# Two MLPs of a hybrid decoder step in seven block products instead of eight, over four chunks of 272 tokens

## The chip, the cores and the metric

The kernel runs on one core of one Trainium2 chip. The metric is device time in microseconds; the lower the better. TensorE (PE in the profile) multiplies matrices into the accumulator, VectorE (DVE), ScalarE (ACT) and GpSimd (POOL) work on elements, and the queue of SyncE (SP) issues most transfers between DRAM and the on-chip memory.

## The reference

One inference step of a two-layer decoder over 1088 tokens: 1024 of a prompt and 64 of eight samples, width 1024. Layer 0 has a state-space mixer, layer 1 attention with forget gates over shared keys and values; both attend to a memory as well. Each layer ends with an MLP of inner width 4096, which is what the change is about:

```python
def rmsnorm(x, g):
    x32 = x.astype(jnp.float32)
    y = x32 * lax.rsqrt(jnp.mean(x32 * x32, axis=-1, keepdims=True) + RMS_EPS)
    return (y * g.astype(jnp.float32)).astype(x.dtype)

def sqrelu_mlp(x, w_up, w_down):
    h = jax.nn.relu(x @ w_up)
    return (h * h) @ w_down
...
        h = h + jnp.concatenate([y_main, y_mem], axis=-1) @ p["w_out"][i]
        h = h + sqrelu_mlp(rmsnorm(h, p["norm_mlp"][i]), p["w_up"][i], p["w_down"][i])
    y = rmsnorm(h, p["norm_final"])
```

Everything is 32-bit floating point.

## The kernel before

Activations lie with the channel on the partitions and the tokens along the row: `[128, 8, w]` for 1024 channels and a chunk of w tokens. There are three chunks (`CH`, line 19): 384, 384 and 320 tokens.

A product keeps 32-bit accuracy by parts. `split` (line 186) writes the operand rounded for the tensor engine, H, with ACT (line 191), and the rest, L, with DVE (line 192, POOL in some places). `mm3` (line 181) then does three matmuls, H·H, H·L and L·H, into one bank of the accumulator; all matmuls go through `mm` at line 179. `Weights` loads a block of 1024 words a partition into one of four raw places `wf` and splits it into a pair of the eight places `wr`; `wall` goes round all four.

`dense` (line 210) takes up to four output tiles of 128 channels: it loads and splits their weights, then goes chunk by chunk, tile by tile, 8 k-tiles by 3 matmuls each, and hands the bank to `evict`. Banks 0 and 1 take turns. `tick` after each tile runs work that `defer` has put off, so that a norm falls behind matmuls that are already in PE's queue.

`mlp` (line 307) runs over 8 groups of 512 hidden channels. Up: four tiles by `dense`; `ev_up` takes the relu (ACT, line 314), squares (POOL, line 315) and splits the tile into `hids`, which stay on the chip. Down: four blocks of weights, and for each chunk 8 output tiles of 4 k-tiles by 3 matmuls, added by DVE (line 329) to the residual stream `hs[c]`. In the last group the squares for the next norm are summed as the tiles come (`add_square`, line 1011), and `done` norms a finished chunk.

Before it, `out_proj` (line 299) makes the 8 tiles of the output projection in two `dense` calls; at the end of the second each chunk is normed by `norm_later` (line 260): sums of squares at once, and `rest` two tiles later, with the gains applied on DVE (line 255) and a split. After the first MLP `xn` is normed with the gains of layer 1's mixer, and `xk_later` (line 1056) norms the same chunks once more with the gains of the shared keys and values.

The order of instructions on each engine's queue comes from a scheduler that simulates the program; engines then work their queues in order. Storage is laid out by hand: `setA` holds the residual stream, `setB` and `setC` the two parts of normed activations, and `phase` gives a stage its own area, which is where `hids` lie.

Of the kernel before, what the change touches and what calls it, by code (L numbers as in the profile page):

```python
# [18 lines left out]
CH = ((0, 384), (384, 384), (768, 320))  # L19
# [25 lines left out]
def yoco_step(ctx: ExitStack, tc: tile.TileContext, I, O, upto=99, dbg=None):  # L45
# [17 lines left out]

    class Place:
        """words from lo to hi of a tile"""

        def __init__(self, tile_, lo, hi):
            self.t, self.o, self.hi = tile_, lo, hi
# [10 lines left out]
        def at(self, shape, dt=F32):  # L79
            n = math.prod(shape[1:])  # L80
            assert self.o + n <= self.hi, (shape, self.o, self.hi)
            return shaped(self.t[0:shape[0], self.o:self.o + n], shape, dt)
# [7 lines left out]
    class Ring:  # L90
        """places used in turn"""
# [8 lines left out]
    class Banks:  # L100
        """banks of the accumulator, used in turn"""
# [9 lines left out]
    F_WORDS = 720 + SET + 4 * WT + 3 * 768 + 3 * 384 + 4 * 432  # L111
    R_WORDS = 2 * SET + 8 * WT
    P_WORDS = SB_WORDS - F_WORDS - R_WORDS
    top = Place(sb.tile([128, F_WORDS], F32, name="plain", tag="plain"), 0, F_WORDS)
    rnd = Place(sb.tile([128, R_WORDS], F32R, name="rounded", tag="rounded"), 0, R_WORDS)
    phases = ExitStack()
    ctx.enter_context(phases)

    def phase(name, plain, rounded=0):
        """storage of a phase, which takes the place of the one before"""  # L120
        phases.close()
        pool = phases.enter_context(tc.tile_pool(name=name, bufs=1, reuse_waits="tile"))
        assert plain + rounded <= P_WORDS, (plain + rounded, P_WORDS)
        r = []
        for n, d in ((plain, F32), (rounded, F32R)):
            r.append(Place(pool.tile([128, n], d, name=f"{name}_{d.name}", tag=d.name), 0, n) if n else None)
        return r
# [15 lines left out]
    sq0 = top.words(3 * 768)  # L143
    sq = Ring([sq0.sub(768 * i, 768) for i in range(3)])
    rs0 = top.words(3 * 384)
    rsr = Ring([rs0.sub(384 * i, 384) for i in range(3)])
    nt0 = top.words(4 * 432)
# [11 lines left out]
    class Weights:  # L159
        """raw weights and their two parts, by turns"""  # L160
# [4 lines left out]
        def __call__(self, src, shape, e=V):  # L165
# [3 lines left out]
            SY.dma_start(out=raw, in_=src)  # L169
            split(H, L, raw, e)  # L170
# [6 lines left out]
    # ------------------------------------------------------------ helpers  # L177
# [32 lines left out]
    def dense(srcs, xs, evict, load=wall, nk=8, done=None, each=tick):  # L210
        """weights stationary, activations moving; groups of tiles run chunk by chunk"""
# [48 lines left out]
    def norm_later(h, c, gi, out, keep=None, lag=2):  # L260
        """statistics now, the rest when a few more tiles have been handed to the tensor engine"""
        w = CH[c][1]
        s1 = rms_sums(h, w)

        def rest():
            rs = rms_scale(s1, w)
            if keep is not None:
                keep[c] = rs
            out[c] = rms_apply(h, rs, gi, c)
        defer(lag, rest)  # L270

# [27 lines left out]
    def out_proj(ys, w, hs, done):  # L299
        for g in range(2):  # L300
            def ev(i, c, ps, w_, g=g):
                r = hs[c][:, 4 * g + i, :]
                V.tensor_tensor(r, ps, r, op=ALU.add)
# [3 lines left out]
    def mlp(l, hs, xs, done, each=None):  # L307
        _, ph = phase(f"mlp{l}", 0, 8 * T)
        hids = {(i, c): ph([128, 2, w], F32R) for c, (_, w) in enumerate(CH) for i in range(4)}
        ebank = Banks([2, 3, 4, 5, 6])  # L310
        for g in range(8):
            def ev_up(i, c, ps, w):
                r = nt([128, w])
                S.activation(r, ps, AF.Relu)  # L314
                G.tensor_tensor(r, r, r, op=ALU.mult)  # L315
                split(hids[i, c][:, 0, :], hids[i, c][:, 1, :], r)

            dense([I["w_up"][l, 4 * g + i] for i in range(4)], xs, ev_up)
            W = [wall(I["w_down"][l, g, i], [128, 4, 256]) for i in range(4)]
            for c, (t0, w) in enumerate(CH):  # L320
                for m in range(8):
                    H, L = W[m // 2]
                    ms = slice(128 * (m % 2), 128 * (m % 2) + 128)
                    ps = ebank([128, 512])
                    for k in range(4):
                        x = hids[k, c]
                        mm3(ps[:, :w], H[:, k, ms], L[:, k, ms], x[:, 0, :], x[:, 1, :], k == 0, k == 3)
                    r = hs[c][:, m, :]
                    V.tensor_tensor(r, ps[:, :w], r, op=ALU.add)  # L329
                    if g == 7 and each:  # L330
                        each(r, c, m)
                    tick()
                if g == 7:
                    done(hs[c], c)
# [1122 lines left out]
    for c in range(3):  # L1457
        load_ym(1, c)
# [145 lines left out]
```

## Time and profile before

| | |
|---|---|
| median of three runs | 2814.22 us (2812.74, 2817.23, 2814.22) |
| span of the profiled execution | 2812.6 us |
| PE busy | 2690.6 us (96%), 17669 matmuls |
| DVE, ACT, POOL busy | 1345.2, 944.0, 681.5 us |
| moved by DMA | 307.06 MB, mean 109 GB/s |
| first MLP, second MLP | about 440 to 1220 us, about 1970 to 2795 us of the span |

The profiled execution's own time is its span, 1.6 us under the median of the runs, so the two can be compared directly. The page gives busy time, share and number of instructions of each engine, 40 slices of the span, and the chain of work that ended last. A group's line reads: line of the kernel, engine, operation, output<-inputs, shape, count | busy time, mean duration of one in ns | idle time of that engine before them and what ended it. Matmuls overlap in the pipeline, so the price of one in a row is busy time over count, not the mean duration. In the table of stretches a column is busy time and, in brackets, the number of instructions.

### The profile page before, as it was taken

Reading aid. Unit: us, or ns where it says so; the run is one execution under the profiler, and the core shown is the slowest. Engines: PE = TensorE matmul, PEld = TensorE weight load, DVE = VectorE, ACT = ScalarE, POOL = GpSimd, SP = SyncE. Lnnn points to the kernel's source line nnn. Section 1 sums busy time; section 2 is a strip of 40 time slices with the busy share of each in tenths; the row PEclk is TensorE's granted clock in tenths of the full one; section 3 lists DMA queues with packets and bytes.
Section 4 is the critical chain, followed back from the end, with each engine's and each line's share of the span. In section 5 each row is a group of like instructions: output and inputs, shape, how many; then the busy total and the mean of one; then the engine's idle time right before and its main releaser. Section 6 shows DMA issues by size and latency. Waiting matters only on the chain.

```text
span 2812.6 us, 45335 instructions
## 1 busy us (share of the span) xinstructions
PE 2690.6 (96%) x17669; PEld 2526.0 (90%) x17669; DVE 1345.2 (48%) x2597; ACT 944.0 (34%) x1947; POOL 681.5 (24%) x776
## 2 busy tenths in 40 slices
PE   7787999999999999999999989999999999999997
PEld 6776889999999999998889766777999999999997
DVE  8899646432323232283523477785553232233225
ACT  6332533221122122244422466773232122211224
POOL 6487211110111011121101455540011011101113
PEclk9899999999999999999999999999999999999999
DMA  6435332010101111132586898885211111111101
GB/s 205 111 105 171 99 108 77 31 61 31 61 31 53 38 52 39 46 131 83 182 266 211 269 293 299 277 292 179 77 31 53 38 51 40 45 45 39 52 31 64
DMA packets 175293, 307.06 MB, mean 109 GB/s; under 512 B 42661, under 2 KB 103398, under 8 KB 173542
## 3 DMA queue, kind: packets, MB, share of 16 engines
q1 hardware_dynamic: 152486, 294.46, 32.3%
q10 hardware_dynamic: 22080, 8.92, 1.2%
q8 instruction: 139, 2.28, 0.3%
q0 software_dynamic: 512, 0.79, 0.1%
q14 instruction: 76, 0.62, 0.1%
HBM read 259.18 MB, written 44.93 MB: 108 GB/s over the span
## 4 chain that ended last, share of the span: by engine, by line
PE 81%; DVE 9%; DMA 3%; POOL 2%; ACT 2%; issue 2%; SPq 0%; POOLq 0%; ACTq 0%; DVEq 0%
PE banks L179 79%; DVE rounded L192 2%; PE banks L1327 1%; DVE plain L255 1%; ACT rounded L191 1%; DMA layer_float<-in_cache_v 1%; POOL logf_float L989 1%; DVE plain L862 1%; ACT plain L1313 1%; DMA plain<-qtscr 0%; DVE plain L870 0%; POOL rounded L192 0%; PE banks L469 0%; DVE plain L1019 0%; POOL plain L864 0%
## 5 line engine op out<-in xcount | busy, mean ns | idle before, releaser
L179 PE MATMUL banks<-rounded 128*128 128x384 f32 (+4 forms) x8918 | 1548.3, 331 | 64.8 <-ACT rounded L191 16.7
L179 PEld LDWEIGHTS banks<-rounded 128*128 128x128 f32 x8918 | 1460.2, 191 | 111.9 <-issue 22.1
L179 PE MATMUL banks<-mlp_float32r,rounded 128*128 128x384 f32 (+1 forms) x4608 | 769.7, 328 | 0.0
L179 PEld LDWEIGHTS banks<-mlp_float32r,rounded 128*128 128x128 f32 x4608 | 763.1, 188 | 1.1
L191 ACT ACTIVATE rounded<-plain 128x1024 fp32r<-128x1024 f32 (+6 forms) x379 | 306.6, 821 | 784.8 <-PE banks L179 675.7
L315 POOL TENSOR_TENSOR plain<-plain 128x384 f32<-128x384 f32 (+1 forms) x192 | 202.6, 1055 | 1390.6 <-ACT plain L314 1276.8
L329 DVE TENSOR_TENSOR plain<-banks,plain 128x384 f32<-128x384 f32 (+1 forms) x384 | 204.6, 533 | 382.1 <-PE banks L179 382.1
L192 DVE TENSOR_TENSOR rounded<-plain,rounded 128x1024 fp32r<-128x1024 f32 (+4 forms) x252 | 293.8, 1172 | 152.1 <-ACT rounded L191 149.7
L192 DVE TENSOR_TENSOR mlp_float32r<-plain,mlp_float32r 128x384 fp32r<-128x384 f32 (+1 forms) x192 | 102.8, 535 | 485.0 <-ACT mlp_float32r L191 485.0
L314 ACT ACTIVATE plain<-banks 128x384 f32<-128x384 f32 (+1 forms) x192 | 89.7, 467 | 289.5 <-PE banks L179 286.0
L192 POOL TENSOR_TENSOR rounded<-plain,rounded 64x512 fp32r<-64x512 f32 (+5 forms) x127 | 144.7, 1148 | 163.0 <-ACT rounded L191 160.2
L191 ACT ACTIVATE mlp_float32r<-plain 128x384 fp32r<-128x384 f32 (+1 forms) x192 | 97.4, 507 | 211.6 <-POOL plain L315 211.6
L179 PE MATMUL banks<-layer_float 128*32 128x256 f32 (+2 forms) x1104 | 98.2, 370 | 11.2 <-ACT layer_float L1149 4.3
L192 DVE TENSOR_TENSOR rounded<-banks,rounded 128x512 fp32r<-128x512 f32 (+2 forms) x136 | 85.9, 636 | 25.3 <-ACT rounded L191 23.6
L191 ACT ACTIVATE rounded<-banks 128x512 fp32r<-128x512 f32 (+2 forms) x136 | 74.8, 559 | 57.9 <-PE banks L1327 32.9
L1317 POOL TENSOR_SCALAR plain<-plain 128x640 f32<-128x640 f32 (+6 forms) x96 | 71.4, 747 | 77.9 <-DVE plain L1316 39.1
L179 PE MATMUL banks<-rounded,layer_float32r 128*128 128x256 f32 x480 | 87.6, 299 | 2.5 <-ACT rounded L191 1.4
L1313 ACT ACTIVATE plain<-banks,plain 128x512 f32<-128x512 f32 (+2 forms) x144 | 82.3, 576 | 17.8 <-DVE plain L1310 9.5
L179 PEld LDWEIGHTS banks<-rounded,layer_float32r 128*128 128x128 f32 x480 | 68.9, 190 | 15.5 <-ACT rounded L191 4.1
L179 PEld LDWEIGHTS banks<-layer_float 128*32 128x32 f32 (+1 forms) x1104 | 39.6, 113 | 45.6 <-issue 8.9
L1307 DVE TENSOR_REDUCE plain<-banks 128x1 f32<-128x384 f32 (+3 forms) x144 | 76.6, 550 | 6.3 <-PE banks L179 5.0
L255 DVE SCALAR_TENSOR_TENSOR plain<-plain 128x384 f32<-128x384 f32 (+1 forms) x120 | 74.9, 674 | 7.2 <-DMA ymscr<-plain 5.7
(318 smaller groups left out, 1784.8 us busy)
## 6 DMA issues: line engine op xcount, KB each, us to landing
plain<-in_cache_kT SPq DMA_DIRECT2D x128, 384.0 KB
layer_float<-in_cache_v SPq DMA_DIRECT2D x128, 384.0 KB
plain<-in_w_up SPq DMA_DIRECT2D x64, 512.0 KB
plain<-in_w_down SPq DMA_DIRECT2D x64, 512.0 KB
plain<-in_w_in SPq DMA_DIRECT2D x16, 512.0 KB
plain<-in_w_out SPq DMA_DIRECT2D x16, 512.0 KB
plain<-in_xT SPq DMA_DIRECT2D x4, 1536.0 KB
plain<-fpast SPq DMA_DIRECT2D x8, 768.0 KB
```

Of the source, the lines that this page charges most:

```text
L179: PE.matmul(out, a, b, start=first, stop=last)
L191: S.activation(H, src, AF.Copy)
L192: e.tensor_tensor(L, src, H.bitcast(F32), op=ALU.subtract)
L255: V.scalar_tensor_tensor(t[:, j, :], h[:, k, :], gains[:, gi, k:k + 1], rs, op0=ALU.mult, op1=ALU.mult)
L314: S.activation(r, ps, AF.Relu)
L315: G.tensor_tensor(r, r, r, op=ALU.mult)
L329: V.tensor_tensor(r, ps[:, :w], r, op=ALU.add)
L862: V.tensor_tensor_scan(X[:, r, a], m8, X[:, r, a], 0.0, op0=ALU.mult, op1=ALU.add)
L989: G.indirect_dma_start(out=fp[i // 8][:, 128 * (i % 8):128 * (i % 8) + 128], out_offset=None, in_=I["logf_rows"], in_offset=bass.IndirectO ...
L1307: V.tensor_reduce(st[:, i:i + 1], ps[:, :n], axis=AX.X, op=ALU.max, negate=True)
L1313: S.activation(pf[:, k0:k0 + n], ps[:, :n], AF.Exp, bias=st[:, 0:1], accum_out=st[:, 2 + i:3 + i])
L1317: G.tensor_scalar(pf[:, 0:L], pf[:, 0:L], st[:, 4:5], 0.0, op0=ALU.mult, op1=ALU.add)
```

## The change

A product of two matrices cut into 2 x 2 blocks takes eight block products; Strassen's scheme takes seven, between sums and differences of blocks. The change does this for both products of the MLP, with the hidden channels or output channels, the inner dimension and the tokens each cut in two.

- There are four chunks of 272 tokens in the whole kernel; an operand holds two of them (`g`).
- `mlp_norm` replaces `norm_later`: it stores the residual chunk to DRAM (`hmid`), norms in place, and makes from two pairs of chunks the seven moving operands, already split, which stay on the chip for all of the up stage.
- Up: 16 rounds of 256 hidden channels. `weight_ops` loads 1 MB of weights, forms four sums on POOL and splits seven operands. `seven` runs the products in turn over three pairs of banks. `to_hidden` forms the seven operands of the down stage from the four result blocks and stores them to DRAM (`hops`) through three places; the last two rounds are stored as they are (`hcnv`).
- Down: 7 blocks of 512 hidden channels by 4 sweeps of 7 products, operands read back from DRAM into eleven places; results are gathered in `H5`, on DVE and POOL. The residual comes back with POOL in blocks 1 to 4. The eighth block is done in the old way with `hcnv`, and feeds `each` and `done`.
- The gains of layer 1's mixer and of the shared keys and values are multiplied into the raw weights on POOL (`Weights`, `gain`), so there is one norm after the first MLP and `xk_later` is gone.
- The sums over the past's log-forget values run between the two halves of the output projection (`past_sums`), not after it.

The core of the diff:

```diff
-CH = ((0, 384), (384, 384), (768, 320))
+CH = ((0, 272), (272, 272), (544, 272), (816, 272))
...
             SY.dma_start(out=raw, in_=src)
+            if gain is not None:
+                G.tensor_tensor(raw, raw, gain[:, :, None].broadcast_to(shape), op=ALU.mult)
             split(H, L, raw, e)
...
+    def operands(b11, b12, b21, b22, extra, put, which=(0, 1, 2)):
+        if 0 in which:
+            put(0, b11)
+        if 2 in which:
+            put(2, b21)
+        if 1 in which:
+            V.tensor_tensor(b11, b12, b11, op=ALU.subtract)
+            V.tensor_tensor(extra, b22, b11, op=ALU.subtract)
+            put(1, extra)
+            put(3, b11)
+            V.tensor_tensor(b12, b22, b12, op=ALU.subtract)
+            put(4, b12)
+            put(5, b22)
+            V.tensor_tensor(b21, b21, extra, op=ALU.subtract)
+            put(6, b21)
...
+    def weight_ops(src, cells, sh):
+        n = turn["w"]
+        turn["w"] += 1
+        raw = raws2[n % 2]
+        raw = raw.at([128, *src[1]])
+        SY.dma_start(out=raw, in_=src[0])
+        a11, a12, a21, a22 = cells(raw)
+        at = ((0, 7, 1)[n % 3], 2, 3, 4, 5, 6, (1, 0, 7)[n % 3])
+        r = [wr[j].at([128, 2, *sh], F32R) for j in at]
+
+        def put(i, x):
+            split(r[i][:, 0], r[i][:, 1], x)
+
+        put(0, a11)
+        put(6, a22)
+        G.tensor_tensor(a22, a21, a22, op=ALU.add)
+        G.tensor_tensor(a21, a11, a21, op=ALU.subtract)
+        G.tensor_tensor(a11, a22, a11, op=ALU.subtract)
+        put(1, a11)
+        put(2, a12)
+        put(3, a22)
+        G.tensor_tensor(a12, a12, a11, op=ALU.subtract)
+        put(4, a21)
+        put(5, a12)
+        return r
+
+    def seven(lhs, rhs, nk, gs, tmp, out):
+        s1, u2, u4 = (t[:, gs] for t in tmp)
+
+        def product(i):
+            n = turn["bank"] = (turn["bank"] + 1) % 3
+            v = shaped(banks[:, 1024 * n:1024 * n + 1024], [128, 2, 512], F32)[:, :, 0:CN]
+            for g in range(gs.start, gs.stop):
+                for k in range(nk):
+                    mm3(v[:, g], *lhs(i, k), *rhs(i, g, k), k == 0, k == nk - 1)
+            return v[:, gs]
+
+        S.activation(s1, product(0), AF.Copy)
+        V.tensor_tensor(u2, product(1), s1, op=ALU.add)
+        out(0, 0, product(2), s1)
+        V.tensor_tensor(u4, product(3), u2, op=ALU.add)
+        p = product(4)
+        out(1, 1, p, u4)
+        V.tensor_tensor(u2, p, u2, op=ALU.add)
+        out(0, 1, product(5), u4)
+        out(1, 0, product(6), u2)
...
+    def mlp_norm(h, c, gi):
+        w = CH[c][1]
+        s1 = rms_sums(h, w)
+        SY.dma_start(out=hmid[c], in_=h)
...
+        def rest():
+            rs = rms_scale(s1, w)
+            for k in range(8):
+                V.scalar_tensor_tensor(x[:, k, :], h[:, k, :], gains[:, gi, k:k + 1], rs,
+                                       op0=ALU.mult, op1=ALU.mult)
...
+            operands(x0[:, 0:4], x[:, 0:4], x0[:, 4:8], x[:, 4:8], extra, put, (1,) if c % 2 else (0, 2))
+        defer(2, rest)
...
+        hl = Ring([setA[i].sub(1088 * j, 1088) for i, j in ((2, 1), (0, 0), (0, 1))])
+        def to_hidden(j, q, extra):
+            b, kp = j // 2, j % 2
+            def put(i, x):
+                t = hl([128, 2, 2, CN], F32R)
+                split(t[:, 0], t[:, 1], x)
+                SY.dma_start(out=hops[i][b][:, kp], in_=t.rearrange("p h g n -> p h (g n)").bitcast(F32))
...
+        W = up_weights(0)
+        for j in range(16):
...
+            for gs in (slice(0, 1), slice(1, 2)) if j == 0 else (slice(0, 2),):
+                def out(m, n, ps, u):
+                    x = q[m][n][:, gs]
+                    V.tensor_tensor(x, ps, u, op=ALU.add)
+                    S.activation(x, x, AF.Relu)
+                    S.activation(x, x, AF.Square)
+                seven(..., 4, gs, tmp, out)
...
+            if j < 15:
+                W = up_weights(j + 1)
+            to_hidden(j, q, tmps(sh))
...
+        for b in range(7):
+            ops = hidden(b)
+            for d in range(2):
+                W = down_weights(b, d)
+                if d == 0 and 0 < b < 5:
+                    hr = residual.at([128, 8, CN])
+                    SY.dma_start(out=hr, in_=hmid[b - 1])
+                for e in range(2):
+                    m0 = 4 * d + 2 * e
+                    def out(m, n, ps, u):
+                        h = H5[:, :, n, m0 + m, :]
+                        if b == 0:
+                            V.tensor_tensor(h, ps, u, op=ALU.add)
+                            return
+                        V.tensor_tensor(h, ps, h, op=ALU.add)
+                        G.tensor_tensor(h, h, u, op=ALU.add)
+                    seven(..., 2, slice(0, 2), [tmps(sh) for _ in range(3)], out)
+                    if 0 < b < 5:
+                        for m in range(m0, m0 + 2):
+                            hc = hs[b - 1][:, m, :]
+                            G.tensor_tensor(hc, hc, hr[:, m, :], op=ALU.add)
...
-    xk = [None] * 3
-
-    def xk_later(c):
-        xk[c] = rms_apply(hs[c], rs[c], 4, c)
```

More of the change, by code (lines that the diff above doesn't have):

```diff
@@ L258, in rms_apply @@
         return H, L
[L260 to L270, printed above, removed]
     def expacc(out, x, t, ni):
@@ L297, in dump_c, with out_proj @@
             SY.dma_start(out=dbg[name][:, :, CH[c][0]:CH[c][0] + CH[c][1]], in_=ap)
-    def out_proj(ys, w, hs, done):
+    def out_proj(ys, w, hs, done, between=None):
         for g in range(2):
+            if g and between:
+                between()
             def ev(i, c, ps, w_, g=g):
@@ L305, in out_proj @@
             dense([w[4 * g + i] for i in range(4)], ys, ev, done=(lambda c: done(hs[c], c)) if g else None)
[L307 to L334, printed above, removed]
@@ new lines, in yoco_step @@
+    hops = [dt_(f"hops{i}", [7, 128, 2, 2, 2 * CN]) for i in range(7)]
+    hcnv = dt_("hcnv", [4, 128, 2, T])
+    hmid = [dt_(f"hmid{c}", [128, 8, w]) for c, (_, w) in enumerate(CH)]
+    raws2 = [joined(wf[2 * i:2 * i + 2]) for i in range(2)]
+    turn = {"w": 0, "bank": 0}
+    xplace, Pq = [None, None], []
+    def operands(b11, b12, b21, b22, extra, put, which=(0, 1, 2)):
[13 more added lines that the diff above has]
+            put(6, b21)
@@ L599, in yoco_step @@
     mem_values_of(1, kvr, wv1)
-    norm0(1)
-    norm0(2)
+    for c in range(1, NC):
+        norm0(c)
     def tiny(dt=F32):
@@ L969, in yoco_step @@
             next(mem, None)
[L970 removed]
+        n = 34 if c < NC - 1 else 26
         for m in range(6):
@@ L1004, in yoco_step @@
         return
-    xn, rs = [None] * 3, [None] * 3
-    sums = [sq.p[2].sub(384 * (c % 2), 384) for c in range(3)]
+    xl = [joined(x).at([128, 8, T], F32R) for x in (setB, setC)]
+    xn = [[x[:, :, t0:t0 + w] for x in xl] for t0, w in CH]
+    sums = [sq.p[2].sub(384 * (c % 2), 384) for c in range(NC)]
     two = Ring(sq.p[0:2])
@@ L1050, in ev_q1, with gained @@
         SY.dma_start(out=qtscr[i0 + i][:, CH[c][0]:CH[c][0] + n], in_=t[:, 0:n])
-        if c == 2:
-            SY.dma_start(out=qsscr[i0 + i], in_=t[:, 256:320])
-    xk = [None] * 3
-    def xk_later(c):
-        xk[c] = rms_apply(hs[c], rs[c], 4, c)
-    dense([I["w_in1"][6], I["w_in1"][7]], xn, ev_qm)
+        if c == NC - 1:
+            SY.dma_start(out=qsscr[i0 + i], in_=t[:, SAM])
+    def gained(gi):
+        return lambda src, shape: wall(src, shape, gain=gains[:, gi, :])
+    dense([I["w_in1"][6], I["w_in1"][7]], xn, ev_qm, gained(1))
     fa, fr = phase("layer1", P_WORDS - 3072, 3072)
@@ L1068, in yoco_step @@
     i0 = 0
-    dense([I["w_in1"][i] for i in range(4)], xn, ev_q1, each=mem_tick)
+    dense([I["w_in1"][i] for i in range(4)], xn, ev_q1, gained(1), each=mem_tick)
     i0 = 4
-    dense([I["w_in1"][i] for i in (4, 5)], xn, ev_q1, done=xk_later, each=mem_tick)
+    dense([I["w_in1"][i] for i in (4, 5)], xn, ev_q1, gained(1), each=mem_tick)
     for _ in mem:
@@ L1179, in yoco_step @@
     for j in range(3):
-        W = [wall(I["w_vf"][j, kh], [128, 4, 260]) for kh in range(2)]
+        W = [wall(I["w_vf"][j, kh], [128, 4, 260], gain=gains[:, 4, 4 * kh:4 * kh + 4]) for kh in range(2)]
         for b in range(9):
             t0 = 128 * b if b < 8 else 960
-            c = min(t0 // 384, 2)
-            ls_ = slice(t0 - CH[c][0], t0 - CH[c][0] + 128)
+            ls_ = slice(t0, t0 + 128)
             ps = dbank([128, 512])
@@ L1256, in yoco_step @@
     for i in range(6):
-        dense([I["w_k"][i]], xk, lambda _, c, ps, w, i=i: ev_k(i, c, ps, w), each=lambda: step(RATE[1]))
-    hlr = [Ring([x[c].sub(6 * CH[c][1], 512) for c in range(3)]) for x in (setB, setC)]
+        dense([I["w_k"][i]], xn, lambda _, c, ps, w, i=i: ev_k(i, c, ps, w), gained(4), each=lambda: step(RATE[1]))
+    hlr = [Ring([x[c].sub(6 * CH[c][1], 512) for c in range(NC)]) for x in (setB, setC)]
     wfl = joined(wf[2:4])
```

248 lines of the change are left out of this document (174 added, 74 removed).

## The prediction

> **What bounds the kernel now.** I read the page first (busy shares, slices, chain), then the table of stretches, then the groups of instructions of each engine.
>
> ```profile
> span 2812.6 us, 45335 instructions
> PE 2690.6 (96%) x17669; PEld 2526.0 (90%) x17669; DVE 1345.2 (48%) x2597; ACT 944.0 (34%) x1947; POOL 681.5 (24%) x776
> ...
> GB/s 205 111 105 171 99 108 77 31 61 31 61 31 53 38 52 39 46 131 83 182 266 211 269 293 299 277 292 179 77 31 53 38 51 40 45 45 39 52 31 64
> ...
> PE 81%; DVE 9%; DMA 3%; POOL 2%; ACT 2%; issue 2%; SPq 0%; POOLq 0%; ACTq 0%; DVEq 0%
> ```
>
> PE is busy 96% of the span and 81% of the chain that ended last, so what counts is which stage gives PE less to do and whether something else then ends its waits. The two MLPs are the calm slices of the GB/s row, 7 to 17 and 29 to 40; the table of stretches shows them in microseconds:
>
> ```profile
> core 0: us, PE busy (x) PEld busy (x) DVE busy (x) ACT busy (x) POOL busy (x), PEclk, DMA share, GB/s
> ...
> 460.00:1200.00 740.00, 740.00 (x4479) 739.58 (x4478) 254.78 (x387) 174.09 (x278) 100.99 (x96) 1.00 0.14 46
> ...
> 1990.00:2760.00 770.00, 770.00 (x4648) 769.31 (x4647) 265.13 (x407) 180.48 (x287) 101.63 (x96) 1.00 0.13 42
> ```
>
> PE never stops there at full clock; DVE stands at 34%, POOL at 14%, the DMA at 46 GB/s. Only fewer or shorter matmuls shorten this, and there is room beside them. How long one matmul takes, from the groups with shapes kept apart and one row of the timeline:
>
> ```profile
> L179 PE MATMUL banks<-rounded 128*128 128x384 f32 x5184 | 960.5, 343 | 34.1 <-ACT plain L820 11.3 <-DVE rounded L192 10.3 <-ACT rounded L191 3.5
> L179 PE MATMUL banks<-mlp_float32r,rounded 128*128 128x384 f32 x3072 | 544.8, 338 | 0.0
> ...
> L179 PE MATMUL banks<-mlp_float32r,rounded 128*128 128x320 f32 x1536 | 227.5, 308 | 0.0
> ...
> 1460.63 6.04 PE L179 MATMUL banks<-rounded 128*128 128x260 f32 x48
> ```
>
> They are pipelined, so the price is busy time over count, in the MLP rows: 177.3 ns for 384 columns, 148.1 for 320, hence 0.456 ns a column, and 126.2 ns for 272. The last row gives at most 126 ns for 260 columns: short matmuls with a new stationary tile each pay no visible floor there.
>
> The Trainium skill (TensorE: Matmul & The Clock Gate, "Back-to-back issue gap") gives N / 2.4 GHz + 2.5 ns, 115.8 ns here as an estimate; its 162.5 for 384 columns is 15 ns under the trace, so the sum stays with the rows. By the page it would come out 113 us lower (10,848 matmuls by 10.4 ns).
>
> **The matmuls.** Before, each layer has 32 x 8 x 3 x 3 = 2304 up and as many down; the rows above are the down half of both layers, 772.3 us, so one layer's MLP costs 772.3. After: up 16 rounds x 7 products x 2 halves x 4 k x 3 parts = 2688, down 28 sweeps x 7 x 2 x 2 x 3 = 2352, and the eighth hidden block in the old way, 4 x 8 x 4 x 3 = 384. 5424 x 126.2 ns = 684.5: 87.8 us less a layer, if PE stays the bound. A round is 21.2 us of PE, a sweep 10.6.
>
> **What is laid on the other engines.** The rows for it:
>
> ```profile
> L192 DVE TENSOR_TENSOR rounded<-plain,rounded 128x1024 fp32r<-128x1024 f32 x172 | 214.2, 1245 | 129.4 <-ACT rounded L191 127.3 <-DMA out_v<-plain 1.1 <-PE banks L179 0.9
> L329 DVE TENSOR_TENSOR plain<-banks,plain 128x384 f32<-128x384 f32 x256 | 142.3, 556 | 307.9 <-PE banks L179 307.9
> L192 DVE TENSOR_TENSOR rounded<-banks,rounded 128x512 fp32r<-128x512 f32 x120 | 81.7, 684 | 19.6 <-ACT rounded L191 18.2
> L192 DVE TENSOR_TENSOR mlp_float32r<-plain,mlp_float32r 128x384 fp32r<-128x384 f32 x128 | 71.3, 557 | 421.0 <-ACT mlp_float32r L191 421.0
> L329 DVE TENSOR_TENSOR plain<-banks,plain 128x320 f32<-128x320 f32 x128 | 62.4, 487 | 74.1 <-PE banks L179 74.1
> ```
>
> About 1.05 ns an element and 150 ns: 272 is 0.44 us, 512 0.69, 544 0.72, 1088 1.29, from PSUM or SBUF alike. An up round on DVE: 7 products evicted (544) 5.0, 7 halves of weights split (512) 4.8, 4 subtractions and 7 splits of hidden operands (544) 7.9; 17.8 us beside 21.2 of PE. ACT:
>
> ```profile
> L191 ACT ACTIVATE rounded<-banks 128x512 fp32r<-128x512 f32 x120 | 70.7, 596 | 38.5 <-PE banks L1327 32.9 <-DVE plain L1307 2.6 <-DVE rounded L192 0.9
> ```
>
> 23 operations of 512 or 544 at 0.60 to 0.63, 14 us: covered. POOL:
>
> ```profile
> L192 POOL TENSOR_TENSOR rounded<-plain,rounded 64x512 fp32r<-64x512 f32 x48 | 61.0, 1277 | 51.8 <-ACT rounded L191 50.3 <-PE banks L179 0.5 <-DVE plain L1316 0.3
> L192 POOL TENSOR_TENSOR rounded<-plain,rounded 64x256 fp32r<-64x256 f32 x36 | 26.2, 728 | 38.5 <-ACT rounded L191 37.6
> ```
>
> Elements per partition count: 1.28 us for 512, 0.76 for 272, 1.34 for 544. A round's four weight sums are 5.1 us. A down sweep in blocks 1 to 4 has four adds into h (5.4), half of four weight sums (2.6), two residual adds (1.5): 9.5 us beside 10.6 of PE; blocks 5 and 6 have 8.0, block 0 2.6. DVE there has 7 x 0.72 + 3.5 x 0.69 = 7.4.
>
> DVE and POOL disturb each other. The timeline of the last norm:
>
> ```profile
> 2773.57 0.55 DVE L1019 TENSOR_TENSOR plain<-plain 128x384 f32<-128x384 f32 x1
> ...
> 2774.67 8.84 POOL L1483 TENSOR_TENSOR plain<-plain 128x384 f32<-128x384 f32 x8 [22.97 <-DVE plain L245]
> ...
> 2778.19 1.15 DVE L1019 TENSOR_TENSOR plain<-plain 128x384 f32<-128x384 f32 x1 [0.65 <-ACT plain L1018]
> ...
> 2779.27 0.55 DVE L329 TENSOR_TENSOR plain<-banks,plain 128x384 f32<-128x384 f32 x1
> ```
>
> The same SBUF operation takes 0.55 us alone and 1.15 beside POOL; the one that reads PSUM stays at 0.55. Lower bound for a round: no disturbance, PE's 21.2. Upper: whatever reads SBUF twice on DVE excludes POOL, 12.7 + 5.1 + 5.0 = 22.8. I take the middle, 22.0: DVE at half speed during 60% of POOL's 5.1 us plus its own stretch is 19.8, under PE, but an in-order queue at 93% will hold an eviction back at times (three pairs of banks give it two products, 6 us). A sweep of blocks 1 to 4: 10.6, or with exclusion 9.5 + 2.4 = 11.9; middle 11.2. The others 10.6, covered. Up 16 x 22.0 = 352; down 12 x 10.6 + 16 x 11.2 = 306; the last block 48.5.
>
> **Moved and added DMAs.** A round stores 7 tiles of 557 KB and loads 1 MB, 4.9 MB in 22 us = 225 GB/s; a block of down reads 7 x 1.11 + 2 + 1.1 MB in 44 us = 250. The page's slices reach 299, so bandwidth covers it. Eleven places for seven operands let four come a block early; the other three have the last sweep. The sync queue takes 8 issues a round: seven stores that wait for DVE's splits and, among them, the load of the next weights, which is late if a store ahead of it waits; it has a round and a half of lead (two raw places). If the cover of the stores fails, DVE's queue stops at a split, and behind that stand the evictions that free PE's banks: third rival.
>
> **Start of each MLP.** Before, a chunk's norm hides behind the next chunk's 16.8 us of matmuls. Now the chunk also becomes operands. The norm's pieces:
>
> ```profile
> 459.02 0.56 DVE L243 SCALAR_TENSOR_TENSOR plain<-banks,plain 128x384 f32<-128x384 f32 x1
> ...
> 460.60 3.27 DVE L255 SCALAR_TENSOR_TENSOR plain<-plain 128x384 f32<-128x384 f32 x6
> ```
>
> At 272: evictions 1.7, sums 2.6, finish 1.6, gain 8 x 0.43 = 3.5, then two splits of 1088 for an even chunk (12.0 in all), four subtractions and five splits for an odd one (21.1). 66 us of DVE against 48.4 of PE in the second half of the output projection, of which the first chunk's 12.1 brings no norm work, and the first weights' 4.8 and 3.0 of evictions come in. DVE ends near 86 us, while PE wants the last operand at 48.4 + 10.6 + 9 = 68: 18 us of stall a layer. Bounds: 3, if DVE's queue is so ordered that only the last chunk's first subtractions show; 25, if the new store of the residual (1.1 MB a chunk, which the norm must wait for because it overwrites h) is not covered by the 12 us between chunks. **Up to down**: 3 us (0 to 8), since h lies where the last stored tiles were.
>
> A layer: 18 + 352 + 306 + 3 + 48.5 = 727.5 against 772.3, 44.8 saved, 89.6 in two.
>
> **The rest.** The other dense products, 5184 - 3072 = 2112 matmuls of 384 and half as many of 320, become 4224 of 272: 533.1 - 530.8 = +2.3. Folding gains into the weights adds 20 POOL operations of about 2.3 us on the engine that the page shows least busy, and drops one norm on DVE; neither ended PE's waits: 0 (-5 to +5). Before the first MLP every chunk-wise instruction comes four times instead of three: some 20 DVE operations of the first norm at 0.15 us of fixed price more, and stores of 136 bytes a row instead of 192: +3 (-3 to +10). The running sums of the past (two scans, a copy, two subtractions on DVE, two stores on the sync queue) move between the halves of the output projection; their wait for the gathers is already in DVE's queue:
>
> ```profile
> 437.12 2.35 DVE L994 TENSOR_TENSOR_SCAN logf_float<-plain,logf_float 96x1024 f32<-96x1024 f32 x1 [5.99 <-DMA logf_float<-in_logf_rows,plain]
> ```
>
> Earlier in the queue it may hold evictions back for these 6 us once more; the gathers end when they did, so between 0 and 6 I take 0. The tail after the last matmul, 11 us long, handles 272 columns instead of 320: -2.
>
> ```profile
> 2800.56 0.82 PE L179 MATMUL banks<-plain 128*128 128x320 f32 x2 [3.38 <-DVE plain L1019]
> ```
>
> Sum: 2812.6 - 89.6 + 2.3 + 3 - 2 = 2726.3. The median of the runs is 1.6 above this execution's span: **2728 us**.
>
> **Rivals.**
> *PE keeps the bound and nothing stalls.* For: everything is under PE on paper. Against: DVE's 18 us start. Only 3 us a layer lost: 2814.2 - 2 x 84.8 + 3 = **2648**.
>
> *DVE and POOL shut each other out* (the 0.55 to 1.15 row). Rounds 22.8, sweeps 11.9: 18 + 365 + 318 + 3 + 48.5 = 752.5; 2814.2 - 39.6 + 3 = **2778**. The Trainium skill (GPSIMD Engine Reference, "Specifications") names this as one SBUF interface shared with VectorE, in contention when VectorE has two SBUF inputs; the row agrees, as PSUM operations keep their time.
>
> *The stores hold DVE: slower.* The hidden operands go through three places, and a split waits for the store three before. The nearest transfer, 512 KB:
>
> ```profile
> 1690.77 4.47 DMA plain<-qtscr
> ...
> 1745.99 5.48 DMA plain<-qtscr
> ```
>
> 5.5 plus ACT and DVE 1.35 is 6.9 us a turn, 2.3 a tile, where DVE has 1.1 us of work: 1.2 us of waiting on four to seven tiles, 4.7 to 8.2 a round, on a queue with 1.4 to spare. Rounds of 24.5 to 28; at 26 the layer costs 791.5, the kernel **2856**. It decides from a round of 24.7 us: (772.3 - 375.5 - 1.6) / 16. Against it: those waits can be filled with weight splits and evictions.
>
> **How the numbers follow.** Forecast (2690 to 2765) 0.48, no stall 0.14, exclusion 0.15, stores 0.20, others 0.03. 0.2% is 5.6 us, the spread of the runs shown (2812.74 to 2817.23). Faster 0.48 + 0.14 + 0.14, slower 0.19 + 0.02, same 0.03. 2650 to 2850 leaves out the tip of the first rival and half of the last.
>
> **What would show it.** Matmuls of 272 at 126 ns; 18 us of holes at the start of each MLP, ended by DVE; rounds of 22 us with DVE above 85%; POOL above 85% in sweeps of 11 us. Wrong, if a round is over 24.7 with DVE waiting for ACT and ACT for stores, or if matmuls of 272 cost over 135 ns.

## The result and the profile after

| | before | after | ratio |
| --- | --- | --- | --- |
| median of the runs, us | 2815.72 (2812.74 to 2817.4) | 2762.1 (2759.31 to 2765.74) | 0.9818, 95% interval 0.9801 to 0.9835 |
| span of the profiled execution, us | 2812.6 | 2759.2 | |

1.8% faster: 54 us by the medians, 53 by the spans, where 86 were forecast. The same program run once more against the kernel before gave 0.9805 (0.9789 to 0.9822), with a span of 2751.1. The page of the kernel after; the chain's shares are those of the chain that ended last:

```profile
span 2759.2 us, 54020 instructions
PE 2575.1 (93%) x20345; PEld 2404.4 (87%) x20345; DVE 2023.4 (73%) x3421; ACT 1239.9 (45%) x2544; POOL 1249.9 (45%) x1142
...
GB/s 200 109 110 165 105 122 83 82 248 229 234 241 314 208 258 266 198 157 108 147 261 218 265 303 312 305 296 159 96 88 249 230 236 238 306 238 242 280 170 65
...
PE 56%; DVE 18%; POOL 9%; DMA 8%; issue 4%; ACT 4%; another core or an unknown queue 1%; SPq 0%; POOLq 0%; ACTq 0%; DVEq 0%
```

PE lost 116 us of busy time, the span only 53, and PE fell from 81% of the chain to 56%. The calm slices of 31 to 64 GB/s are now at 208 to 314 for the most part. Where the MLP is bound, by the table of stretches of the kernel after (the start, a steady stretch of up, the middle of the passage to down, a steady stretch of down):

```profile
core 0: us, PE busy (x) PEld busy (x) DVE busy (x) ACT busy (x) POOL busy (x), PEclk, DMA share, GB/s
...
480.00:500.00 20.00, 16.12 (x121) 15.41 (x120) 20.00 (x25) 10.74 (x16) 12.53 (x4) 0.96 0.14 57
500.00:540.00 40.00, 29.79 (x155) 27.52 (x153) 39.12 (x59) 17.40 (x27) 7.32 (x4) 0.76 0.15 55
540.00:700.00 160.00, 160.00 (x1271) 159.88 (x1271) 147.60 (x196) 102.57 (x179) 49.09 (x30) 1.00 0.62 238
...
860.00:870.00 10.00, 4.35 (x23) 3.98 (x23) 1.97 (x4) 1.89 (x4) 0.00 (x0) 0.69 1.01 420
870.00:880.00 10.00, 6.96 (x34) 6.35 (x33) 1.45 (x2) 0.66 (x1) 0.00 (x0) 0.67 1.03 416
...
930.00:1060.00 130.00, 127.03 (x998) 125.00 (x997) 102.53 (x125) 32.65 (x54) 127.18 (x94) 1.00 0.64 249
```

Four regimes. At the start of the MLP (480 to 540) DVE is busy for 59.1 of 60 us and PE stands at times; in up's rounds PE never stops, and 160.00 / 1271 is 125.9 ns a matmul, with DVE at 92%; between up and down only the DMA is full; in down POOL is at 98% and PE still at 98%.

Read by sections, for the second half of the output projection and the MLP behind it. Their ends are marked in the timelines by evictions and by first copies, ACT's copies of the first product of a round or sweep:

| section, us | forecast | layer 0 | layer 1 |
| --- | --- | --- | --- |
| second half of the projection, rounds 0 and 1 (the start) | 110.4 | 119.6 | 118.9 |
| 13 rounds of up | 286.0 | 278.7 | 276.6 |
| first copy of the last round to that of the third sweep (the passage) | 44.6 | 58.7 | 57.3 |
| 26 sweeps of down | 285.2 | 281.2 | 282.2 |
| the eighth hidden block | 47.0 | 52.2 | 46.8 |
| together | 773.2 | 790.4 | 781.8 |
| before | 816.3 by rows | 809.1 | 810.2 |

The forecasts are the prediction's terms cut at these marks: 45.4 of projection, 18 of stall, two rounds of 22.0 and a product of 3; 13 x 22.0; 6/7 of a round, 3, two sweeps of 10.6 and 1.5; 10 x 10.6 + 16 x 11.2; 48.5 less the first group. In the kernel before the sections run from 439.4 to 1248.5 and from 1988.0 to 2798.2 us of its span, which the table of the time before gives only roughly. Both layers together are 26 us over the forecasts and were 13 cheaper before than the rows said; everything outside them is 6 us shorter instead of some 0.5 longer. That is the 33 us between the forecast's span, 2726.3, and 2759.2.

The passage is the term that failed. It holds 324 matmuls, 324 x 125.9 ns = 40.8 us; 17 us a layer are lost there, where the prediction had 3. Waits of PE in that place, then one of ACT, timelines of the kernel after:

```profile
862.38 1.89 PE L208 MATMUL banks<-rounded 128*128 128x272 f32 x12 [2.27 <-DMA rounded<-hops]
867.65 3.06 PE L208 MATMUL banks<-rounded 128*128 128x272 f32 x12 [3.38 <-DMA rounded<-hops]
872.93 2.16 PE L208 MATMUL banks<-rounded 128*128 128x272 f32 x12 [2.22 <-DMA rounded<-hops]
...
873.61 0.66 ACT L220 ACTIVATE plain<-plain 128x544 fp32r<-128x544 f32 x1 [11.60 <-DMA hcnv<-plain]
```

In the first layer PE waits 7.9 us for loads of operands and 5.6 for DVE and ACT, and ACT waits 11.6 for a store of the eighth hidden block. That names the transfers, not the cause: it may be their order, the amount, or what they wait for.

### The profile page after: what moved, and what is told of

It reads as the page before. It is cut to its first block, busy times and chain, and to the rows that moved or that the text cites. A ratio compares the mean times of both kernels' runs of the same rounds, so it can differ in the third digit from the quotient of the medians.

```text
span 2759.2 us, 54020 instructions
## 1 busy us (share of the span) xinstructions
PE 2575.1 (93%) x20345; PEld 2404.4 (87%) x20345; DVE 2023.4 (73%) x3421; ACT 1239.9 (45%) x2544; POOL 1249.9 (45%) x1142
## 4 chain that ended last, share of the span: by engine, by line
PE 56%; DVE 18%; POOL 9%; DMA 8%; issue 4%; ACT 4%; another core or an unknown queue 1%; SPq 0%; POOLq 0%; ACTq 0%; DVEq 0%
PE banks L208 54%; DVE rounded L221 5%; POOL plain L539 4%; DMA hops<-plain 2%; DVE plain L221 2%; DMA rounded<-hops 2%; PE banks L1558 1%; POOL plain L547 1%; ACT rounded L220 1%; POOL plain L381 1%; POOL plain L379 1%; POOL plain L380 1%; ACT plain L220 1%; POOL plain L385 1%
## 5 line engine op out<-in xcount | busy, mean ns | idle before, releaser
L208 PE MATMUL banks<-rounded 128*128 128x272 f32 (+4 forms) x11552 | 1626.2, 296 | 97.6 <-ACT rounded L220 27.7
L220 ACT ACTIVATE rounded<-plain 128x512 fp32r<-128x512 f32 (+5 forms) x575 | 384.3, 679 | 641.5 <-PE banks L208 473.2
L221 DVE TENSOR_TENSOR rounded<-plain,rounded 128x512 fp32r<-128x512 f32 (+4 forms) x520 | 490.8, 954 | 107.4 <-ACT rounded L220 103.3
L208 PE MATMUL banks<-mlp,rounded 128*128 128x272 f32 x3840 | 526.2, 292 | 18.0 <-DVE plain L536 5.4
L208 PEld LDWEIGHTS banks<-mlp,rounded 128*128 128x128 f32 x3840 | 502.1, 191 | 24.2 <-DVE rounded L221 8.0
L379 POOL TENSOR_TENSOR plain<-plain 128x512 f32<-128x512 f32 x60 | 98.5, 1642 | 709.2 <-DVE rounded L221 709.2
L539 POOL TENSOR_TENSOR plain<-plain,flex 128x544 f32<-128x544 f32 x192 | 292.0, 1531 | 42.0 <-DVE plain L538 39.3
L221 DVE TENSOR_TENSOR plain<-plain 128x544 fp32r<-128x544 f32 x212 | 209.8, 1006 | 28.0 <-ACT plain L220 21.9
L220 ACT ACTIVATE plain<-plain 128x544 fp32r<-128x544 f32 x212 | 136.6, 653 | 187.9 <-DMA hops<-plain 103.6
L538 DVE TENSOR_TENSOR plain<-banks,plain 128x544 f32<-128x544 f32 x192 | 137.7, 718 | 57.7 <-PE banks L208 54.9
L385 POOL TENSOR_TENSOR plain<-plain 128x512 f32<-128x512 f32 x60 | 101.1, 1685 | 65.6 <-DVE rounded L221 65.0
L221 POOL TENSOR_TENSOR rounded<-plain,rounded 64x512 fp32r<-64x512 f32 (+2 forms) x55 | 77.4, 1414 | 67.4 <-ACT rounded L220 61.9
L381 POOL TENSOR_TENSOR plain<-plain 128x512 f32<-128x512 f32 x60 | 101.1, 1685 | 3.0
L221 DVE TENSOR_TENSOR rounded<-banks,rounded 128x512 fp32r<-128x512 f32 (+2 forms) x136 | 86.0, 637 | 15.1 <-ACT rounded L220 13.2
L380 POOL TENSOR_TENSOR plain<-plain 128x512 f32<-128x512 f32 x60 | 93.2, 1553 | 4.7
```

Of the source, the lines that this page charges most:

```text
L208: PE.matmul(out, a, b, start=first, stop=last)
L220: S.activation(H, src, AF.Copy)
L221: e.tensor_tensor(L, src, H.bitcast(F32), op=ALU.subtract)
L379: G.tensor_tensor(a22, a21, a22, op=ALU.add)
L380: G.tensor_tensor(a21, a11, a21, op=ALU.subtract)
L381: G.tensor_tensor(a11, a22, a11, op=ALU.subtract)
```

## The experiments

Ratios are to the kernel before on the same chip in the same minutes; "passage" is the section of the table, layer 0 / layer 1.

| kernel | median, us | ratio (95%) | passage | start |
| --- | --- | --- | --- | --- |
| after, again | 2758.2 | 0.9805 (0.9789 to 0.9822) | 57.0 / 59.4 | 119.2 / 118.9 |
| loads in order | 2755.6 | 0.9802 (0.9781 to 0.9823) | 58.9 / 59.0 | 119.5 / 118.9 |
| wide rows | 2761.3 | 0.9815 (0.9794 to 0.9837) | 63.2 / 62.0 | 119.1 / 119.4 |
| plain MLP | 2820.6 | 1.0038 (1.0026 to 1.0050) | | |
| two places | 2770.6 | 0.9851 (0.9830 to 0.9871) | 61.9 / 62.7 | 118.3 / 118.4 |
| free place | 2764.2 | 0.9820 (0.9804 to 0.9836) | 59.3 / 62.4 | 119.1 / 119.0 |
| stores first | 2735.4 | 0.9721 (0.9705 to 0.9737) | 46.9 / 47.4 | 119.4 / 118.8 |
| splits on POOL | 2768.3 | 0.9835 (0.9818 to 0.9851) | 58.1 / 59.8 | 122.9 / 122.9 |
| stores first, sums on DVE | 2730.0 | 0.9717 (0.9699 to 0.9734) | 47.9 / 46.8 | 114.9 / 114.8 |
| stores first, fourth place | 2765.4 | 0.9841 (0.9823 to 0.9858) | 60.9 / 61.8 | 119.2 / 118.9 |
| both | 2756.9 | 0.9813 (0.9794 to 0.9831) | 61.8 / 61.2 | 114.9 / 115.4 |
| all, stores in order | 2732.9 | 0.9723 (0.9704 to 0.9741) | 47.7 / 45.5 | 114.9 / 115.6 |

**Is the gain the algorithm's?** The eight block products put back, all else as changed (the `mlp` of the kernel before, with its `rms_apply` norm, over four chunks).

> The four chunks of 272 tokens, the gains in the weights and everything else of the change stay, but both MLPs go by the eight block products of the kernel before, so this run is the change without Strassen's algorithm. By the prediction's terms the MLPs then cost 2 x 3.1 us more than before (3072 x 126.2 ns = 387.7 a half against 386.15), the other dense products 2.3, the front 3, the tail -2: 2816 + 9.5 = 2825 us, and Strassen's algorithm itself is worth 2825 - 2762 = 63. By the traces' milestones (front +4.9, mixer of the second layer -10.7, tail -0.9) it is 2815, and the algorithm is worth 53. Rival (the gain is not the algorithm's but that of the smaller chunks and the folded gains): 2790 or below.

1.0038: 10.7 us slower than the kernel before, by the prediction's terms 9.5. So the four chunks, the folded gains and the rest cost in sum what they were said to cost; their terms one by one were not measured. The seven products alone are worth 62 to 66 us (1.0038 less 0.9818 or 0.9805) of the 89.6 forecast, and what is missing is missing inside the MLPs.

**The order of the loads.** `after(x)` makes the scheduler issue an instruction behind x; the rest of the edit only declares `last`.

```diff
-                SY.dma_start(out=t.bitcast(F32), in_=hops[i][b])
+                with after(last[0] if b < 2 else None):
+                    last[0] = SY.dma_start(out=t.bitcast(F32), in_=hops[i][b])
```

> Undoes nothing; the seven operand loads of down's first block, and those of the second behind them, are only put into the sync queue in the order in which the sweep uses them. Theory (order): the stall between up and down comes from operands 5 and 6 and two of the next block being loaded ahead of 2, 3 and 4. The first two sweep intervals (24.9 + 18.6 us in the first layer, 23.1 + 17.8 in the second) fall to about 13 + 12, some 17 us a layer: 2762 - 34 = 2728 us. Rival (bandwidth): 7.8 MB at the 407 GB/s seen there take 19 us in whatever order; the two intervals keep a sum of 38 or more and the time stays above 2752.

The first sweep did shrink, from 24.9 to 7.6 us; the second grew to 32.1, and the passage stayed at 59. My theory fell. Timelines of this kernel, sync queue, DVE and PE:

```profile
846.76 4.88 SPq L515 DMA_DIRECT2D mlp<-hops  x4
...
860.81 15.85 SPq L477 DMA_DIRECT2D hcnv<-plain  x6
...
879.93 1.36 DVE L537 TENSOR_TENSOR plain<-banks,flex 128x544 f32<-128x544 f32 x2 [10.99 <-DMA hcnv<-plain]
...
880.71 3.09 PE L208 MATMUL banks<-mlp,rounded 128*128 128x272 f32 x12 [14.00 <-DVE plain L537]
```

Now one row says what the order hid. PE waits 14.0 us for DVE, and DVE 11.0 us for a store of the eighth hidden block: its sums go into h, which lies on the places of the last stored tiles. Its last six stores were issued from 860.81 on, behind eleven loads of 1.11 MB, of which four belong to the second block, the first residual (1.11 MB) and the next weights (1.05): 14.4 MB. From 840 us on the DMA of this kernel runs at 399 to 419 GB/s, 16.4 MB in 40 us, and reaches them near 880.

**Wider rows in that place.** The eighth block's halves apart in DRAM, one store of 2176-byte rows instead of two of 1088; the bytes stay the same.

```diff
-    hcnv = dt_("hcnv", [4, 128, 2, T])
+    hcnv = dt_("hcnv", [4, 2, 128, 2, 2 * CN])
...
```

> The eighth hidden block lies in DRAM with the two token halves apart, so that its stores go in rows of 2176 bytes, half as many of them, instead of 1088, and its loads in two pieces of 2176. Theory (order of the loads): nothing changes in the order, so the first two sweep intervals after up keep a sum of about 42 us and the time stays within 5 us of 2762. Rival (bandwidth and packets): these stores are what fills the DMA in that stretch; the two intervals lose 5 to 8 us a layer, 2748 us.

The passage did not shrink (63.2 / 62.0) and the time is that of the kernel after, so wider rows do not remove the stall: here too a sum of DVE into h waits for a store of the eighth block, 12.0 us in the first layer. The scheduler placed other work anew with this edit, so the 4 us more are not explained.

**The store that gates h, two ways.** Let the last round's tiles avoid the first sweeps' words:

```diff
+        last2 = Ring([hl.p[2], hl.p[0]])
...
-                    t = hl([128, 2, 2, CN], F32R)
+                    t = (last2 if j == 15 else hl)([128, 2, 2, CN], F32R)
```

> As the kernel with the loads in order, and the four stored tiles of up's last round go through the two places that the first two sweeps of down don't write, instead of all three. There DVE's first sum into h (L537) waited 11.0 us for a store of the eighth block that stood behind eleven loads in the DMA. Theory (a store gates h): the last round's first copy to the third sweep's first copy, 58.9 us in the kernel with the loads in order, falls to 43 to 46, as nothing else is late: 13 us a layer, 2755.6 - 26 = 2729 us. Rival (bandwidth: 16 MB at 410 GB/s take until 880 us in any case and the sweeps need them): the stall appears one or two sweeps later, less than 10 us in all, 2746 or above.

or let the stores leave first:

```diff
-                        SY.dma_start(out=to[:, i, :, n], in_=t[:, i].bitcast(F32))
+                        stored[0] = SY.dma_start(out=to[:, i, :, n], in_=t[:, i].bitcast(F32))
...
+            if b == 1:
+                last[0] = stored[0]
...
-                    SY.dma_start(out=hr, in_=hmid[b - 1])
+                    with after(stored[0]):
+                        SY.dma_start(out=hr, in_=hmid[b - 1])
```

> As the kernel with the loads in order, and the second block's loads and the first residual load stand behind the last store of the eighth hidden block in the sync queue. Theory (a store gates h, and it was queued behind 5.6 MB that nothing needs yet): the store lands 5.6 MB / 0.41 MB per us = 13 us sooner; the stretch from the last round's first copy to the third sweep's falls from 58.9 to about 47 to 49 us, 2755.6 - 21 = 2735 us. Rival (bandwidth): the second block's operands come late instead and the fifth sweep waits; less than 8 us in all.

The first gained nothing: with two places the last splits wait for the same stores, ACT first, DVE behind it, and DVE's sums behind that (timelines of the kernel with the free place, ACT and DVE):

```profile
884.59 0.66 ACT L220 ACTIVATE plain<-plain 128x544 fp32r<-128x544 f32 x1 [12.01 <-DMA hcnv<-plain]
...
885.43 0.73 DVE L221 TENSOR_TENSOR plain<-plain 128x544 fp32r<-128x544 f32 x1 [11.19 <-DMA hcnv<-plain]
```

The wait was moved from one reader of the stores to another. The second came out at 2735.4 against a forecast of 2735, with a passage of 46.9 / 47.4 (47 to 49 expected). Timelines of the kernel with the stores first:

```profile
853.59 13.01 SPq L477 DMA_DIRECT2D hcnv<-plain  x6
866.65 2.58 SPq L518 DMA_DIRECT2D mlp<-hops  x2
...
871.06 1.34 DVE L541 TENSOR_TENSOR plain<-banks,flex 128x544 f32<-128x544 f32 x2
...
871.83 3.06 PE L208 MATMUL banks<-mlp,rounded 128*128 128x272 f32 x12 [2.91 <-DVE plain L541]
```

Counted from the last round's first copy (836.7 and 838.8 us), DVE's sums come 11 us sooner, PE waits 2.9 us instead of 14.0, and the second block's operands are still in time: the sweeps behind it take 10.8 us as before. So 12 us a layer of the 17 were stores waiting behind loads that nothing needed yet. The stores were put first only on top of the loads in order, which alone gained nothing in the passage; without them this was not run.

**What is left of the passage.** A fourth place for the last round's tiles, alone and together with the start's edit below, then with the stores chained among themselves:

```diff
+        last4 = Ring([setA[1].sub(0, 1088), *hl.p])
...
-                    t = hl([128, 2, 2, CN], F32R)
+                    t = (last4 if j == 15 else hl)([128, 2, 2, CN], F32R)
```

> As the kernel with the stores first, and the last round's four stored tiles go through four places, the first of them words of setA that no tile uses any more. There ACT waited 3.6 us for a place, and PE 1.7 behind it. Theory (what is left of that stall, 47 us against 41 without one, is the wait for places): 2 to 3 us a layer less, 2730 us. Rival (the last store itself decides, it lands when the loads and it have gone through): within 2 us of 2735.

> Both of these, the loads in order and the stores first. They act at the two ends of up, so their gains add: if both theories hold 2715 to 2725 us, if only the sums help 2722 to 2729, if neither does 2735 to 2746.

> The last two edits once more, with the last round's stores put in order among themselves, so that the second block's loads really stand behind all of them (in the kernel with the fourth place alone two of the stores came behind those loads, and the stall of 59 us was back). Theory (places): the stretch from the last round's first copy to the third sweep's goes from 47 to 44 or 45 us, 2730 - 5 = 2725 us. Rival (the last store decides, and it lands when the seven loads and it have gone through): 47 us again, 2730.

The first two told something else than asked: 2765 and 2757, the passage back at 61. The edit had changed which store is last in the queue (timelines of the kernel with the fourth place, sync queue and DVE):

```profile
864.93 0.32 SPq L519 DMA_DIRECT2D rounded<-hops  x1
867.57 0.37 SPq L478 DMA_DIRECT2D hcnv<-plain  x1
...
871.75 3.71 SPq L478 DMA_DIRECT2D hcnv<-plain  x2
...
887.13 1.36 DVE L542 TENSOR_TENSOR plain<-banks,flex 128x544 f32<-128x544 f32 x2 [14.67 <-DMA hcnv<-plain]
```

The second block's loads waited for a store that was no longer the last, two stores fell behind them, and the stall returned: the mechanism once more, by accident. With the stores in order the passage is 47.7 / 45.5 and the time 2732.9, no better than without the fourth place, so the places were not it. That the last store decides is not shown either: no engine waits for a store there any more. In the first layer PE waits 3.3 us for operands that are needed and 3.8 us for DVE, and no run separates the two.

**The start: does POOL help DVE?**

```diff
-                split(o[:, 0], o[:, 1], t)
+                split(o[:, 0], o[:, 1], t, G if i in (0, 2, 5) else V)
```

> At the start of each MLP POOL instead of DVE takes the low parts of operands 0, 2 and 5 (six splits of 1088 a layer, 1.28 us each on DVE, about 2.7 on POOL). Theory (DVE and POOL shut each other out on SBUF): what DVE is spared, 7.7 us a layer, it loses beside POOL's 16 us, as its operation of 1088 takes 2.36 instead of 1.28 us there; the time stays within 5 us of 2762 or rises. Rival (DVE alone is the bound there and POOL is free): 6 us a layer less, 2750.

Three splits of seven moved off the engine that is full, and the start is 3.7 to 4 us longer. The other way round, the weight sums of two rounds onto that engine:

```diff
-        raw = raws2[n % 2]
+        raw, E = raws2[n % 2], V if n % 30 < 2 else G
...
-        G.tensor_tensor(a22, a21, a22, op=ALU.add)
+        E.tensor_tensor(a22, a21, a22, op=ALU.add)
```

> As the kernel with the stores first (2735 us), and the weight sums of the first two rounds of each MLP are done by DVE instead of POOL (eight operations of 512, 0.69 us each on DVE, 1.3 to 2.2 and once 6.5 on POOL), so that POOL is silent at the start of the MLP. Theory (DVE and POOL shut each other out): nine operations of DVE there are stretched by 8 us together; without POOL they lose that and DVE gains 5.5 us of work, and the four sums that the first weights wait for end 8 us sooner; 3 to 8 us a layer less, 2720 to 2729 us. Rival (DVE is the bound and POOL only shares the work): 5.5 us a layer more, 2746 us.

5.5 us more work for DVE and a start 4 us shorter, in both layers. The times, 0.9717 and 0.9721, cannot tell the two kernels apart, so that the whole kernel gains is not shown; the section can. Its stretch in the first layer with the sums on POOL (stores first; DVE busy is the third time):

```profile
441.44:560.89 119.45, 105.26 (x743) 102.01 (x742) 103.58 (x159) 57.35 (x92) 26.11 (x12) 0.91 0.29 108
```

and with them on DVE:

```profile
444.20:559.10 114.90, 102.80 (x744) 99.34 (x744) 100.49 (x167) 57.35 (x92) 6.26 (x4) 0.93 0.29 109
```

DVE does 5.5 us more and is busy 3.1 us less: its other operations lost 8.6 us. The same split of 1088 in the timelines of DVE, first of the kernel after run again, beside POOL's sums:

```profile
488.74 2.35 DVE L221 TENSOR_TENSOR mlp<-flex,mlp 128x1088 fp32r<-128x1088 f32 x1
```

and of the kernel with the sums on DVE, POOL silent:

```profile
491.51 1.29 DVE L221 TENSOR_TENSOR mlp<-flex,mlp 128x1088 fp32r<-128x1088 f32 x1
```

The Trainium skill (SBUF — State Buffer, "SBUF: two separate sides") calls the port pair that DVE and POOL share an exclusive lock, held for a whole instruction: whoever comes second blocks. These two runs agree, as the 1.06 us more is nearly one POOL sum of 512 (1.29 us at its shortest). The edit changes a second thing with it: the first weights wait for these sums, the first of which takes 6.50 us on POOL and 0.69 on DVE. How the 4 us divide between the two is not shown.

**How near is the stores' edge?** Two places instead of three in `hl`.

> The stored hidden operands go through two places instead of three. Theory (stores are well covered): a split then waits for the store two before, most of that falls into time that weight splits and evictions fill; rounds go from 21.4 to 22 or 22.5, 10 to 18 us a layer, 2780 to 2800 us. Rival (the stores are at the edge of holding DVE): a turn of 6.9 us over two places is 3.4 us a tile, rounds of 25 or more, 60 us a layer or more, above 2870.

2770.6, below both forecasts: the 13 rounds take 282.7 / 286.6 us instead of 278.7 / 276.6, so 21.7 and 22.0 a round, far from 24.7. ACT's waits for places between 565 and 835 us, of the kernel after:

```profile
ACT plain L220 <- DMA hops<-plain: 58.8, 24, 4.3
```

and of the kernel with two places:

```profile
ACT plain L220 <- DMA hops<-plain: 60.6, 48, 3.9
```

Twice as many waits, the same sum: ACT has the room, and DVE's other work goes on.

## Why the prediction was right or wrong

The direction held, and so did the engine named for the start, DVE. The size missed by 34 us: 2762.1 lies in the forecast's 2690 to 2765, but at its edge.

- **Matmuls of 272 at 126 ns: right.** 125.9 in up's steady stretch. The rule that the prediction weighed (115.8 by the Trainium skill, TensorE: Matmul & The Clock Gate, "Back-to-back issue gap") is stated there for an isolated matmul and does not hold for these; the rows of before did.
- **One layer's MLP before: 6 to 7 us too dear.** 772.3 plus 44.0 for the projection's half stood against a measured 809.1 and 810.2. Busy time over count overstates a pipelined matmul by 0.8%, and a difference of two such sums keeps the error.
- **Up to down, 3 us (0 to 8): the step that failed.** It named the right place ("h lies where the last stored tiles were") and priced it at next to nothing, because bandwidth was taken from averages over a round (225 GB/s) and a block (250). In the passage 11 loads, the stores and two loads of weights meet, 14 MB and more within 40 us, and the DMA is at 382 to 420 GB/s from 850 to 890 us. 17 us, of which 12 are the stores' place in the queue (the kernel with the stores first). About 6 remain, and what decides them stays open.
- **The start, 18 us (3 to 25): too small by 8.** The holes were nearly right, ended by DVE or by ACT, which stood behind DVE and, before the hole at 495 us, behind POOL's sums; waits of PE in this section of the kernel after:

```profile
PE banks L208 <- ACT rounded L220: 7.4, 3, 3.4
PE banks L208 <- DVE plain L408: 2.2, 1, 2.2
PE banks L208 <- DVE rounded L221: 2.2, 2, 1.3
```

  14.1 us with the small ones. But 720 matmuls and four norms' would take 93 us of the 119, so 26 are lost, 12 more than the holes. Most of these go to matmuls that run slowly after a hole. Timeline, then stretches of the kernel after:

```profile
514.19 5.42 PE L208 MATMUL banks<-rounded 128*128 128x272 f32 x23
521.83 4.80 PE L208 MATMUL banks<-rounded 128*128 128x272 f32 x24 [2.21 <-DVE plain L408]
...
512.20:519.00 6.80, 6.20 (x23) 5.47 (x24) 6.66 (x13) 2.80 (x5) 0.00 (x0) 0.50 0.01 2
522.50:525.80 3.30, 3.30 (x17) 3.30 (x16) 3.30 (x4) 2.32 (x5) 3.14 (x3) 0.50 0.00 0
```

  23 matmuls in 5.42 us are 236 ns each, and the granted clock (PEclk, the share of full speed that TensorE was allowed) is 0.50 there. Four such stretches hold 80 matmuls in 18.8 us of PE, 8.8 more than at 125.9 ns; the other 3 us are not explained. The prediction counted each hole once.
- **Rounds of 22.0: pessimistic.** 21.4 and 21.3; between 540 and 838 us PE waits 0.2 us in all. DVE at 92% holds, with three pairs of banks. The disturbance is there, but covered; groups of DVE, kernel after, the same split out of SBUF and out of PSUM:

```profile
L221 DVE TENSOR_TENSOR rounded<-plain,rounded 128x512 fp32r<-128x512 f32 x420 | 374.3, 898 | 71.3 <-ACT rounded L220 69.8
...
L221 DVE TENSOR_TENSOR rounded<-banks,rounded 128x512 fp32r<-128x512 f32 x120 | 81.7, 684 | 12.0 <-ACT rounded L220 10.4
```

  898 ns on average against 684. The *exclusion* rival was right on the engines and wrong on the time, since only the start has no cover. That its 2778 lies nearer to 2762 than the forecast's 2728 is chance: its rounds of 22.8 and sweeps of 11.9 did not come.
- **Sweeps of 10.6 and 11.2: 10.8.** POOL is slower than priced, by its groups in the kernel after:

```profile
L539 POOL TENSOR_TENSOR plain<-plain,flex 128x544 f32<-128x544 f32 x192 | 292.0, 1531 | 42.0 <-DVE plain L538 39.3
```

  1531 ns for the add into h instead of 1.34 us; at 98% it still ends in PE's shadow, and PE waits 3.3 us in 25 sweeps.
- **The stores rival** had the wrong place: three places suffice in the rounds, two nearly do, and it is at the end of up that the stores hold DVE.
- **The rest, 0 to 3 us each: right in sum, by luck.** Front 4.9 (3 forecast). The second layer's mixer 10.7 shorter, of which 5.3 are matmuls of the next stage that already run in the last block's 52.2 us. Against it a new wait in the second layer's projection, which the kernel with the plain MLP has too; DVE, then PE, timelines of the kernel after:

```profile
1939.71 0.79 DVE L323 TENSOR_TENSOR plain<-banks,plain 128x272 f32<-128x272 f32 x2 [5.63 <-DMA plain<-hscr]
...
1940.21 5.13 PE L208 MATMUL banks<-rounded 128*128 128x272 f32 x21 [7.74 <-DVE plain L323]
```

  The residual stream is reloaded too late, 7.7 us that no step had. Why the mixer gained the other 5 us was not tried.
- **past_sums, 0 to 6: not settled.** The stretch differs between two executions of one program. The first half of the projection took 74.6 and 68.3 us (72.3 in the one profile of before), one within the bounds and one below them. Stretches of the kernel after:

```profile
413.00:430.00 17.00, 5.93 (x31) 4.42 (x30) 1.59 (x3) 0.00 (x0) 9.59 (x11) 0.71 0.13 33
```

and of the same kernel again:

```profile
413.00:430.00 17.00, 12.47 (x68) 11.33 (x67) 3.79 (x5) 1.06 (x1) 10.77 (x11) 0.70 0.13 32
```

The two spans differ by 8.1 us, and 6.3 of them lie here. It is not one odd execution: the other kernels of the table, whose front is the same, took 64.5 to 74.8 us for this half. How much of it the median has is not known. For the run again some 15 us of PE busy were expected in this stretch if the stall was one execution's, 6 if it was the program's; 12.47 came, so neither holds.

## What to carry to other kernels

Where two stages meet, add up the bytes that both put into the same queue there, and ask for each store what it stands behind and who waits for the place that it frees: a prefetch issued as soon as its place is free cost 12 us a layer here, twice, and putting loads and stores in order gave it back (0.9818 to 0.9721). A wait moves to the next reader of the same late transfer unless the transfer itself comes earlier. And where DVE was full, POOL was no relief for work on SBUF: see which of the two shortens the stretch, not which has free time.

## What the runs showed of the hardware

- DVE and POOL slowed each other so much that giving DVE 5.5 us more work made the stretch 4 us shorter and DVE's busy time in it 3.1 us less, while giving POOL three of its splits made the stretch 4 us longer.
- At the start holes of 0.3 to 3.5 us, 14.1 us in all, came with 12 us more of loss: matmuls behind them take 200 to 236 ns instead of 126, at a granted clock of 0.50. The Trainium skill (TensorE: Matmul & The Clock Gate, "What's actually happening") gives half clock after an idle window of about 3.4 us. The half agrees, while here shorter holes were enough: the stretch from 522.5 us on follows one of 2.2.
- The stores did not overtake the loads ahead of them in the queue: six of 0.28 MB, issued from 860.81 to 876.7 us behind 14 MB of loads, freed the place that DVE waited for at 879.9.
- While POOL issued sixteen gathers, PE stood for 11 and for 5 of 17 us in two executions of one program, and one eviction of DVE waited 15.1 us for a releaser that the profile does not know. In four other kernels with the same gathers PE was busy for 14.8 to 16.5 of these 17 us, so the gathers alone do not do it. What was waited for stays open.
